# Prompt values of two query tiles in one portion, each head's first scores over 128 keys, and one tile's taps a pair later

## The chip, the cores and the metric

The kernel runs on one core of a Trainium2 chip. A core has a matrix engine (PE, with its weight loads shown apart as PEld), a vector engine (DVE), a scalar engine (ACT), GpSimd (POOL), SyncE (SP), which only issues transfers here, and 16 DMA engines. The metric is the device time of one execution in microseconds. Three runs of the kernel before took 966.77 to 967.02 us, with a median of 966.99 us.

## The reference

One layer of a hybrid decoder is computed for 512 prompt tokens (one sequence) and 8 sequences of 8 sample tokens. Two branches stand side by side, a short gated convolution and a sliding-window attention with 4 key heads of 4 query heads each. Then come a mix by gates, an output projection and a feed-forward part with a convolution of its own. What matters here:

```python
h = _rmsnorm(x, norm1_g) * (1.0 + sc1) + sh1
proj = h @ w_in
b_gate, c_gate, xa, q, k, v, ga, gb = jnp.split(proj, cuts, axis=-1)
u = c_gate * xa
uc, new_conv = _causal_conv(u, conv_buf, conv_w)      # three taps
ya = (b_gate * uc) @ w_conv_out
...
# attention, blocks of 128 queries against the block before and their own
s = einsum('...qhgd,...khd->...hgqk', q, k) * HEAD_DIM ** -0.5 - slope * dist
s = where(valid, s, NEG_INF)          # 0 <= dist <= 128, and no key before the first
m = maximum(max(s), sink);  p = exp(s - m);  p = p / (sum(p) + exp(sink - m))
o = einsum('...hgqk,...khd->...qhgd', p, v)
```

The first block of the prompt has no block before it, so its queries have 128 keys, while those of the other three blocks have 256.

## The kernel before, in words

All activations lie transposed, 128 channels by 576 tokens (512 of the prompt and 64 of the samples). A float32 product is made of float32r matmuls: both operands are split into a high part (ACT writes it as a rounded copy, `whi`, `hh`) and a low part (DVE subtracts, `wlo`, `hl`), and three products are summed in PSUM. A plain product goes through the channels in k-steps of 6 matmuls, each low or high pair once over tokens 0 to 255 and once over tokens 256 to 575 (`128x256` and `128x320` in the rows). From 231 us on most products are made in pairs instead (class `Job`): two output tiles are built from seven products of 288 tokens each, whose weights and operands are sums of the raw ones.

PSUM has two large tiles (`mm`) for products and four banks (`aux`) for all else, taken in turn.

In the stretch that the change touches, seven tiles of the convolution branch (the list `PLAIN`) and the queries and keys of the heads are made by plain products. Attention is woven in between them by a generator, `attention()`: after each k-step a budget is raised, and when it is full the generator runs on to its next `yield`. The text between two yields is called a portion here. There are 16 units, one for each head `hd` and each query tile `i` of 128 queries. Step n of the generator issues

- the scores of unit n (`prompt_scores`): per query head two float32r matmuls, whose stationary tile is 128 queries (the 64 rows of the high and the 64 of the low part of q, one above the other) and whose moving tile is the keys `kh` and then `kl`. Two banks take the four heads. DVE adds the distance term (L1108) and `softmax` follows on DVE and ACT;
- the values of unit n-3 (`prompt_values`): F32 matmuls with V as the stationary tile (L1136) into one bank, which ACT copies to `ot` (L1144). With `i` = 0 there is one key tile (the trace shows 4 records), otherwise two (8 records);
- the turn of unit n-2 (`prompt_turn`): 4 or 8 transposes of the probabilities into one or two banks, which ACT copies to `pt` (L1127).

The queries of head 1, 2 and 3 are made by products among the plain ones (`queries`). ACT scales the high part into `q` (L896), DVE makes `low` (L899), and a POOL transfer `q<-low` (L903) puts it into the other 64 rows. Only then can the scores start that use this `q`.

The order on PE is fixed by the code through the whole of this stretch. DVE and ACT are put in order by a scheduler from its own simulated times until the last plain tile, and from there on they too run as written (`pinned += [pe, act, dve]`). POOL and SP issue the transfers.

In the last plain tile (`at == len(PLAIN) - 1`) the operands of the first pair job are prepared, `jobs[0].prepare("BD")`: B and D are two of the weight operands of the pair, and a letter in the string says that this operand's low half is made by ACT and a POOL transfer (`wlo<-raw`) instead of DVE. `inner[6]` is the convolution of the last plain tile: one tap on ACT and two on DVE (`y<-pad,parT,y`). It runs before the third product of `jobs[0]`; its output is an operand of `jobs[2]`.

Of the kernel before, what the change touches and what calls it, by code (L numbers as in the profile page):

```python
# [16 lines left out]
P = 128  # L17
D = 1024
# [54 lines left out]
def step_kernel(ctx: ExitStack, tc: tile.TileContext, ins: dict, outs: list):  # L73
    nc = tc.nc
# [430 lines left out]
    par = cp.tile([88, P], F32, tag="par", name="par")  # L505
# [298 lines left out]
    for x in range(2):  # L804
        for y in range(2):
            c = slice(2 * y, 2 * y + 2)
# [33 lines left out]
    def vt(i):  # L840
        return V[i // 2][:, i % 2, :]
# [31 lines left out]
    HALF = (slice(0, 64), slice(64, 128))  # L873
    KS, QS, ready = {}, {}, {}
# [12 lines left out]
    def queries(t, ps=None):  # L887
# [55 lines left out]
        op=ALU.mult,  # L943
# [25 lines left out]
    ot = [wp.tile([P, 4, NT], F32, tag="oh", name=nm("o"), bufs=2) for _ in range(2)]  # L969
# [125 lines left out]
    def prompt_scores(hd, i):  # L1095
        w = 256 if i else P
        k0 = (i - 1) * P if i else 0
        ss = [slot("s", shape=[P, 2, 256]) for _ in range(2)]
        kh, kl = (x[:, k0 : k0 + 256] for x in KS[hd])
        for x in range(2):  # L1100
            S = aux()
            for e in range(2):
                q = QS[4 * hd + 2 * x + e][:, i * P : i * P + P]
                dst = S[:, e * 256 : e * 256 + 256]
                matmul(dst, q, kh, start=True, stop=False)
                matmul(dst, q, kl, start=False, stop=True)
            for e in range(2):
                nc.vector.scalar_tensor_tensor(  # L1108
                    out=ss[x][:, e, :w], in0=nd[:, 256 - w : 256],
                    scalar=2.0 ** (-8.0 * (4 * hd + 2 * x + e + 1) / 16),  # L1110
                    in1=S[:, e * 256 : e * 256 + w], op0=ALU.mult, op1=ALU.add,
                )
        softmax(ss, 4, snk[:, 4 * hd : 4 * hd + 4], nsnk[:, 4 * hd : 4 * hd + 4], w)
        return ss
# [13 lines left out]
            pts.append(t)  # L1128
        return pts

    def prompt_values(hd, i, pts):
        nkt = len(pts)
        O = aux()
        for n in range(2 * nkt):
            kt, par = n // 2, n % 2
            done = nc.tensor.matmul(  # L1136
                O[HALF[par], :256],
                vt(i - nkt + 1 + kt)[:, hd * 64 : hd * 64 + 64],
                pts[kt][:, par * 256 : par * 256 + 256],
                start=(kt == 0), stop=(kt == nkt - 1),  # L1140
            )
            if n:
                tc.keep_in_program_order(done)
        nc.scalar.copy(  # L1144
            ot[hd // 2][:, 2 * (hd % 2) : 2 * (hd % 2) + 2, i * P : i * P + P],
            O[:, :256].rearrange("p (g c) -> p g c", g=2),
        )

    def attention():
        units = [(hd, i) for hd in range(4) for i in range(4)]  # L1150
        s, pts = {}, {}
        for n in range(len(units) + 3):
            if n in CACHE_AT:
                cache_load(CACHE_AT.index(n))
            if n < len(units):
                hd, i = units[n]
                while 4 * hd + 3 not in QS or ticks[0] < ready[hd]:
                    yield False
                s[n] = prompt_scores(hd, i)
            yield False  # L1160
            if n >= 3:
                prompt_values(*units[n - 3], pts.pop(n - 3))
            if 2 <= n <= len(units) + 1:
                pts[n - 2] = prompt_turn(units[n - 2][1], s.pop(n - 2))
            yield False
        filler[1] = .35
        before = None
        for n in range(3):
            s, more = [], []
            if n < 2:  # L1170
                yield from decode_scores(n, s, more)
            if before is not None:
                yield from before
            before = decode_values(n, s, more)
# [228 lines left out]
    inner = {}  # L1403
# [7 lines left out]
    def gate_job(n):  # L1411
# [3 lines left out]
    jobs = [  # L1415
        branch(0, 1), branch(2, 4), branch(5, 6), gate_job(0), gate_job(1), gate_job(2), inner_job(3),
        inner_job(7), gate_job(3), branch(3, 7), gate_job(4), gate_job(5), gate_job(6), gate_job(7),
    ]
# [3 lines left out]
    hp = [PairOperands(h, kp, made, xn) for kp in range(4)]  # L1422
# [6 lines left out]
    for at, m in enumerate(PLAIN):  # L1429
        if at in (4, 5):  # L1430
            src, dst = ((ins["cache_k_win"], nks), (ins["cache_v_win"], nvs))[at - 4]
# [12 lines left out]
        w = weights(kpm(w_in, 1024 + m * P), NK)  # L1444
# [13 lines left out]
        w = weights(kpm(w_in, 2048 + m * P), NK)  # L1458
# [4 lines left out]
            jobs[0].load()  # L1463
        if at == len(PLAIN) - 1:
            pinned += [pe, act, dve]
            fs = [f for x in jobs[0].prepare("BD").values() for f in x]
            for k, n in [(0, 2), (1, 1), (2, 1), (3, 1), (4, 2), (5, 1), (6, 1), (7, 1)]:
                steps[k], fs = fs[:n], fs[n:]
            jobs[1].load()
        ps = product(w, h, steps)  # L1470
        u = padded()
# [17 lines left out]
    def g_list(names):  # L1489
        return [g_at(int(n[0]), n[1:]) for n in names.split()]  # L1490

    jobs[0].before = {2: [op.n3 for op in hp], 3: [lambda: inner[6]()]}
    jobs[7].before = {2: [lambda: inner[3]()]}
    jobs[8].before = {2: [lambda: inner[7]()]}
    jobs[9].before = {2: [lambda: state_out(NK, ncv_p[:], ncv_s[:])]}
# [516 lines left out]
    for m0, m1 in FCH:  # L2012
# [31 lines left out]
        if m1 < NF:  # L2044
# [3 lines left out]
            n = m1 - m0  # L2048
# [47 lines left out]
    jobs = [Job(w_dn[FB * P :, :], m * P, made3, lambda m=m: mix_outs(m, 40)) for m in range(0, NK - LATE, 2)]  # L2096
# [139 lines left out]
```

## Time and profile before

| what | value |
|---|---|
| median of three runs | 966.99 us |
| the profiled execution | 968.06 us, its span 966.2 us |
| mean granted TensorE clock | 0.996 |
| PE busy | 950.6 us (98%) |
| DVE busy | 710.5 us (74%) |
| ACT busy | 540.9 us (56%) |
| POOL busy | 131.8 us (14%) |
| share of PE in the chain that ended last | 94% |

The times in the profile are of the profiled execution, and us in a timeline count from the start of its span. A row of a timeline has the start, the duration, the engine, the line, the operation with what it writes and reads (output on the left of `<-`), the shapes, how many instructions were put together, and in brackets the idle time of the engine ahead of it with what ended it. The duration of a matmul includes its way through the array, and matmuls overlap. So what a matmul costs is read from the start of one to the start of the next, and not from its duration. F32 matmuls leave two records for each instruction.

### The profile page before, as it was taken

What the parts mean: (1) busy time and instruction counts of PE and PEld (TensorE: products, weight loads), DVE (VectorE), ACT (ScalarE), POOL (GpSimd) and SP (SyncE); (2) the same over time, 40 slices, a digit from 0 to 9 for tenths busy, and PEclk for the clock granted to TensorE, in tenths of its full rate; (3) what the DMA queues carried; (4) which work ended last, traced back from release to release, by engine and by line L of the source; (5) the groups of instructions that cost most, each with busy time, mean ns of one, the idle gap of its engine ahead of it and who ended that gap; (6) DMA issues with size and microseconds to landing.
All of it is one profiled execution on the core that took longest, in us unless ns stands there. A gap on an engine that the chain in (4) does not pass through costs nothing.

```text
span 966.2 us, 18732 instructions
## 1 busy us (share of the span) xinstructions
PE 950.6 (98%) x7326; PEld 913.5 (95%) x7326; DVE 710.5 (74%) x1330; ACT 540.9 (56%) x1021; POOL 131.8 (14%) x310
## 2 busy tenths in 40 slices
PE   7999999999999999999999999999999999999997
PEld 5799999898899989999889999999999999999997
DVE  4746777687865767876677688995559998968873
ACT  4454665558665446876335567564226565546664
POOL 2222112101211112210001131100000011101110
PEclk8999999999999999999999999999999999999999
DMA  9985332424655768899885742332333333328542
GB/s 276 326 253 147 90 85 71 130 87 119 154 139 160 242 215 214 209 248 268 300 285 131 169 109 66 89 103 73 101 91 93 88 88 103 89 78 175 131 90 99
DMA packets 182794, 144.61 MB, mean 150 GB/s; under 512 B 7704, under 2 KB 162140, under 8 KB 182418
## 3 DMA queue, kind: packets, MB, share of 16 engines
q1 hardware_dynamic: 172546, 111.72, 38.9%
q0 software_dynamic: 10016, 31.44, 14.3%
q8 instruction: 57, 0.93, 0.4%
q14 instruction: 31, 0.25, 0.1%
q10 hardware_dynamic: 144, 0.26, 0.1%
HBM read 113.89 MB, written 12.07 MB: 130 GB/s over the span
## 4 chain that ended last, share of the span: by engine, by line
PE 94%; DVE 2%; DMA 1%; ACT 1%; issue 0%; SPq 0%; POOL 0%; POOLq 0%; DVEq 0%; ACTq 0%
PE mm L112 54%; PE aux L112 37%; PE aux L1232 2%; PE aux L1136 1%; DMA x<-in_x_prompt 1%; DMA q<-low 1%; SPq L497 0%; DVE wlo L112 0%; ACT whi L112 0%; DVE s L1048 0%; ACT hh L112 0%; DVE raw L112 0%; ACT junk L112 0%; DVE hl L112 0%; DVE y L112 0%
## 5 line engine op out<-in xcount | busy, mean ns | idle before, releaser
L112 ACT ACTIVATE whi<-raw 128x1024 fp32r<-128x1024 f32 (+3 forms) x183 | 185.7, 1022 | 104.0 <-PE mm L112 40.9
L112 DVE TENSOR_TENSOR wlo<-raw,whi 128x1024 fp32r<-128x1024 f32 (+3 forms) x159 | 187.3, 1184 | 45.9 <-ACT whi L112 45.1
L112 PE MATMUL mm<-hh,whi 128*128 128x256 f32 x336 | 74.0, 301 | 0.5 <-ACT hh L112 0.5
L112 PE MATMUL mm<-hh,wlo 128*128 128x256 f32 x336 | 71.6, 294 | 0.0
L112 PE MATMUL mm<-hl,whi 128*128 128x256 f32 x336 | 70.8, 295 | 0.1
L112 PE MATMUL aux<-2l,whi 128*128 128x288 f32 (+2 forms) x232 | 68.4, 295 | 0.0
L112 PE MATMUL aux<-2h,whi 128*128 128x288 f32 (+2 forms) x232 | 68.4, 295 | 0.0
L112 PE MATMUL aux<-2h,wlo 128*128 128x288 f32 (+2 forms) x232 | 68.3, 295 | 0.0
L112 DVE TENSOR_TENSOR raw<-raw 128x512 f32<-128x512 f32 x82 | 57.8, 705 | 2.7
L112 PEld LDWEIGHTS mm<-hh,whi 128*128 128x128 f32 x336 | 55.1, 188 | 1.9 <-ACT hh L112 1.1
L112 PEld LDWEIGHTS mm<-hh,wlo 128*128 128x128 f32 x336 | 56.2, 188 | 0.0
L112 PEld LDWEIGHTS mm<-hl,whi 128*128 128x128 f32 x336 | 55.5, 188 | 0.7 <-DVE hl L112 0.5
L112 PE MATMUL aux<-hh,whi 128*128 128x288 f32 (+2 forms) x184 | 53.9, 300 | 0.0
L112 PE MATMUL aux<-hl,whi 128*128 128x288 f32 (+2 forms) x184 | 52.9, 294 | 0.0
L112 PE MATMUL aux<-hh,wlo 128*128 128x288 f32 (+2 forms) x184 | 52.8, 294 | 0.0
L112 PE MATMUL mm<-nh,whi 128*128 128x288 f32 x164 | 48.9, 298 | 0.2 <-DVE g L112 0.2
L112 PE MATMUL mm<-th,whi 128*128 128x288 f32 x164 | 49.1, 300 | 0.0
L112 PE MATMUL aux<-th,whi 128*128 128x288 f32 x164 | 48.6, 296 | 0.0
L112 PE MATMUL mm<-th,wlo 128*128 128x288 f32 x164 | 48.5, 295 | 0.0
L112 PE MATMUL aux<-th,wlo 128*128 128x288 f32 x164 | 48.4, 295 | 0.0
L112 PE MATMUL mm<-nl,whi 128*128 128x288 f32 x164 | 48.4, 295 | 0.0
L112 PE MATMUL mm<-nh,wlo 128*128 128x288 f32 x164 | 48.4, 295 | 0.0
(374 smaller groups left out, 3015.5 us busy)
## 6 DMA issues: line engine op xcount, KB each, us to landing
raw<-in_w_in SPq DMA_DIRECT2D x52, 512.0 KB, 4.9
raw<-in_w_up SPq DMA_DIRECT2D x44, 512.0 KB, 4.0
ada<-in_w_ada SPq DMA_DIRECT2D x64, 256.0 KB, 5.3
wlo<-raw POOLq DMA_DIRECT2D x18, 512.0 KB, 4.6
ad<-in_w_ada SPq DMA_DIRECT2D x32, 256.0 KB, 6.6
raw<-in_w_down SPq DMA_DIRECT2D x16, 512.0 KB, 4.2
sg_dram<-sg POOLq DMA_DIRECT2D x16, 288.0 KB, 4.3
gt<-sg_dram SPq DMA_DIRECT2D x16, 288.0 KB, 5.5
```

Source lines behind the costliest of these rows:

```text
L112: done = getattr(self.engine, name)(*args, **kwargs)
L1136: done = nc.tensor.matmul(O[HALF[par], :256], vt(i - nkt + 1 + kt)[:, hd * 64 : hd * 64 + 64], pts[kt][:, par * 256 : par * 256 + 256], st ...
L1232: done = nc.tensor.matmul(ps[32 * j : 32 * j + 32, :], cT[:, k, :], cols[k][j], start=(k == 1), stop=(k == NK - 2),)
```

## The change

Three things change.

1. `prompt_scores` of a unit with `i` = 0 uses the 128 keys it needs as the moving tile, instead of 256 of which it used 128. This touches 8 matmuls in each of the 4 heads.
2. `prompt_values` takes a list of units. It is called every second step, from n = 4 on, with units n-4 and n-3, two query tiles of the same head. Both go into one bank, columns 0 to 255 and 256 to 511. The two copies on ACT follow behind all matmuls.
3. In the last plain tile the low half of B of `jobs[0]` is made by DVE, and the convolution `inner[6]` runs before the third product of `jobs[1]` instead of `jobs[0]`.

```diff
--- before.py
+++ after.py
@@ -1096,12 +1096,12 @@
         w = 256 if i else P
         k0 = (i - 1) * P if i else 0
         ss = [slot("s", shape=[P, 2, 256]) for _ in range(2)]
-        kh, kl = (x[:, k0 : k0 + 256] for x in KS[hd])
+        kh, kl = (x[:, k0 : k0 + w] for x in KS[hd])
         for x in range(2):
             S = aux()
             for e in range(2):
                 q = QS[4 * hd + 2 * x + e][:, i * P : i * P + P]
-                dst = S[:, e * 256 : e * 256 + 256]
+                dst = S[:, e * 256 : e * 256 + w]
                 matmul(dst, q, kh, start=True, stop=False)
                 matmul(dst, q, kl, start=False, stop=True)
             for e in range(2):
@@ -1128,23 +1128,25 @@
             pts.append(t)
         return pts
 
-    def prompt_values(hd, i, pts):
-        nkt = len(pts)
+    def prompt_values(parts):
         O = aux()
-        for n in range(2 * nkt):
-            kt, par = n // 2, n % 2
-            done = nc.tensor.matmul(
-                O[HALF[par], :256],
-                vt(i - nkt + 1 + kt)[:, hd * 64 : hd * 64 + 64],
-                pts[kt][:, par * 256 : par * 256 + 256],
-                start=(kt == 0), stop=(kt == nkt - 1),
+        for u, (hd, i, pts) in enumerate(parts):
+            nkt, c = len(pts), slice(256 * u, 256 * u + 256)
+            for n in range(2 * nkt):
+                kt, par = n // 2, n % 2
+                done = nc.tensor.matmul(
+                    O[HALF[par], c],
+                    vt(i - nkt + 1 + kt)[:, hd * 64 : hd * 64 + 64],
+                    pts[kt][:, par * 256 : par * 256 + 256],
+                    start=(kt == 0), stop=(kt == nkt - 1),
+                )
+                if u + n:
+                    tc.keep_in_program_order(done)
+        for u, (hd, i, pts) in enumerate(parts):
+            nc.scalar.copy(
+                ot[hd // 2][:, 2 * (hd % 2) : 2 * (hd % 2) + 2, i * P : i * P + P],
+                O[:, 256 * u : 256 * u + 256].rearrange("p (g c) -> p g c", g=2),
             )
-            if n:
-                tc.keep_in_program_order(done)
-        nc.scalar.copy(
-            ot[hd // 2][:, 2 * (hd % 2) : 2 * (hd % 2) + 2, i * P : i * P + P],
-            O[:, :256].rearrange("p (g c) -> p g c", g=2),
-        )
 
     def attention():
         units = [(hd, i) for hd in range(4) for i in range(4)]
@@ -1158,8 +1160,8 @@
                     yield False
                 s[n] = prompt_scores(hd, i)
             yield False
-            if n >= 3:
-                prompt_values(*units[n - 3], pts.pop(n - 3))
+            if n >= 4 and n % 2 == 0:
+                prompt_values([(*units[u], pts.pop(u)) for u in (n - 4, n - 3)])
             if 2 <= n <= len(units) + 1:
                 pts[n - 2] = prompt_turn(units[n - 2][1], s.pop(n - 2))
             yield False
@@ -1463,7 +1465,7 @@
             jobs[0].load()
         if at == len(PLAIN) - 1:
             pinned += [pe, act, dve]
-            fs = [f for x in jobs[0].prepare("BD").values() for f in x]
+            fs = [f for x in jobs[0].prepare("D").values() for f in x]
             for k, n in [(0, 2), (1, 1), (2, 1), (3, 1), (4, 2), (5, 1), (6, 1), (7, 1)]:
                 steps[k], fs = fs[:n], fs[n:]
             jobs[1].load()
@@ -1489,7 +1491,8 @@
     def g_list(names):
         return [g_at(int(n[0]), n[1:]) for n in names.split()]
 
-    jobs[0].before = {2: [op.n3 for op in hp], 3: [lambda: inner[6]()]}
+    jobs[0].before = {2: [op.n3 for op in hp]}
+    jobs[1].before = {3: [lambda: inner[6]()]}
     jobs[7].before = {2: [lambda: inner[3]()]}
     jobs[8].before = {2: [lambda: inner[7]()]}
     jobs[9].before = {2: [lambda: state_out(NK, ncv_p[:], ncv_s[:])]}
```

The order on PE changes in the values and in the shapes of the scores only. In its rows `V` is the value tile, `pt` the transposed probabilities, `s` the scores that are transposed and `ident` the identity; the number behind a name tells one buffer from another, and `x2` means two instructions. The first place is on PE at step n = 4 of the generator (104.6 us in the profile). Before:

```order
L112 MATMUL mm_1355<-hh_352,wlo_1352 128x256
L112 MATMUL mm_1355<-hh_352,wlo_1352 128x320
L1136 MATMUL aux_1368<-pt_1270,V_683 64x256 x2
L112 MATMUL aux_1372<-ident,s_1119 128x128
L112 MATMUL aux_1372<-ident,s_1120 128x128
```

The two value matmuls of the first unit stand between a product and the transposes. The same place on PE now:

```order
L112 MATMUL mm_1355<-hh_352,wlo_1352 128x256
L112 MATMUL mm_1355<-hh_352,wlo_1352 128x320
L112 MATMUL aux_1368<-ident,s_1119 128x128
L112 MATMUL aux_1368<-ident,s_1120 128x128
L112 MATMUL aux_1368<-ident,s_1119 128x128
```

The values are gone, and the product is followed by the transposes at once. On PE one step later, n = 5 (112.4 us), where scores, values and transposes meet, stood before:

```order
L112 MATMUL aux_1449<-kh_1100,q_1337 128x256
L112 MATMUL aux_1449<-kl_1101,q_1337 128x256
L1136 MATMUL aux_1492<-pt_1377,V_683 64x256 x2
L1136 MATMUL aux_1492<-pt_1384,V_683 64x256 x2
L112 MATMUL aux_1498<-ident,s_1195 128x128
L112 MATMUL aux_1498<-ident,s_1196 128x128
L112 MATMUL aux_1498<-ident,s_1195 128x128
L112 MATMUL aux_1498<-ident,s_1196 128x128
L112 MATMUL aux_1449<-kh_1100,q_1338 128x256
```

There were four value matmuls, those of the second unit. And now on PE:

```order
L112 MATMUL aux_1445<-kh_1100,q_1337 128x128
L112 MATMUL aux_1445<-kl_1101,q_1337 128x128
L1137 MATMUL aux_1488<-pt_1270,V_683 64x256 x2
L1137 MATMUL aux_1488<-pt_1373,V_683 64x256 x2
L1137 MATMUL aux_1488<-pt_1380,V_683 64x256 x2
L112 MATMUL aux_1497<-ident,s_1195 128x128
L112 MATMUL aux_1497<-ident,s_1196 128x128
L112 MATMUL aux_1497<-ident,s_1195 128x128
L112 MATMUL aux_1497<-ident,s_1196 128x128
L112 MATMUL aux_1445<-kh_1100,q_1338 128x128
```

The values of the first unit have come to stand ahead of the second's, in the same bank (`aux_1488`), and the scores around them move 128 columns.

The second place is on DVE ahead of `low`, the low part of the last query tile of head 3, from 173 to 179 us in the profile. `den` belongs to the softmax, `nmx` is the negated maximum, L994 scales the probabilities, and `wlo` is the low half of a weight tile. Before:

```order
L991 TENSOR_TENSOR den_2146<-den_2146,es_2147 128x4
L992 RECIPROCAL den_2146<-den_2146 128x4
L1108 SCALAR_TENSOR_TENSOR s_2233<-con_919,aux_2235 128x256 x2
L994 TENSOR_SCALAR s_2126<-s_2126,den_2146 128x256 x2
L994 TENSOR_SCALAR s_2127<-s_2127,den_2146 128x256 x2
L1108 SCALAR_TENSOR_TENSOR s_2234<-con_919,aux_2242 128x256 x2
L975 TENSOR_REDUCE nmx_2249<-s_2233 128x2
L975 TENSOR_REDUCE nmx_2249<-s_2234 128x2
L112 TENSOR_TENSOR wlo_2800<-raw_2797,whi_2799 128x1024
L899 SCALAR_TENSOR_TENSOR low_2279<-mm_2183,q_2280 64x512
```

One scaling stands on each side of an addition to the next scores (L1108). On DVE now:

```order
L991 TENSOR_TENSOR den_2137<-den_2137,es_2138 128x4
L992 RECIPROCAL den_2137<-den_2137 128x4
L994 TENSOR_SCALAR s_2117<-s_2117,den_2137 128x256 x2
L994 TENSOR_SCALAR s_2118<-s_2118,den_2137 128x256 x2
L1108 SCALAR_TENSOR_TENSOR s_2229<-con_919,aux_2231 128x256 x2
L1108 SCALAR_TENSOR_TENSOR s_2230<-con_919,aux_2238 128x256 x2
L975 TENSOR_REDUCE nmx_2245<-s_2229 128x2
L975 TENSOR_REDUCE nmx_2245<-s_2230 128x2
L978 TENSOR_TENSOR nmx_2245<-nmx_2245,nsnk 128x4
L112 TENSOR_TENSOR wlo_2790<-raw_2787,whi_2789 128x1024
L981 TENSOR_TENSOR es_2250<-snk,nmx_2245 128x4
L899 SCALAR_TENSOR_TENSOR low_2275<-mm_2174,q_2276 64x512
```

Both scalings have moved ahead of both additions, and `es` (a small addition) ahead of `low`.

The third place is on DVE in the last plain tile and the first pair jobs, from 226 us on. The preparation of `jobs[0]` before:

```order
L112 TENSOR_TENSOR s_2921<-raw_2912,raw_2914 128x512
L112 TENSOR_TENSOR raw_2914<-raw_2914 128x512
L112 TENSOR_TENSOR wlo_2925<-raw_2912,whi_2924 128x1024
L112 TENSOR_TENSOR raw_2912<-raw_2912,raw_2914 128x512
L112 TENSOR_TENSOR raw_2912<-raw_2912 128x512
L112 TENSOR_TENSOR wlo_3003<-raw_2912,whi_3002 128x1024
```

Its DVE makes two low halves. On DVE now:

```order
L112 TENSOR_TENSOR s_2914<-raw_2905,raw_2907 128x512
L112 TENSOR_TENSOR raw_2907<-raw_2907 128x512
L112 TENSOR_TENSOR wlo_2918<-raw_2905,whi_2917 128x1024
L112 TENSOR_TENSOR wlo_2948<-raw_2907,whi_2947 128x1024
L112 TENSOR_TENSOR raw_2905<-raw_2905,raw_2907 128x512
L112 TENSOR_TENSOR raw_2905<-raw_2905 128x512
L112 TENSOR_TENSOR wlo_2994<-raw_2905,whi_2993 128x1024
```

The second `wlo` in a row is the low half of B. Further on DVE, behind the low parts `hl` of the operands, stood before the taps of `inner[6]`, and behind them the output `g` of the first pair:

```order
L112 TENSOR_TENSOR hl_434<-xn_390,hh_433 128x288
L975 TENSOR_REDUCE nmx_3182<-s_3097 128x2
L112 SCALAR_TENSOR_TENSOR y_3124<-pad_3018,parT,y_3124 128x592 x2
L112 TENSOR_TENSOR raw_2916<-raw_2916,raw_2918 128x512
L112 TENSOR_TENSOR raw_2916<-raw_2916 128x512
L112 TENSOR_TENSOR g_3028<-aux_3030,y_1096 128x288
```

The taps are the row `x2`. They have moved to here on DVE, behind a softmax in the second pair job:

```order
L991 TENSOR_TENSOR den_3172<-den_3172,es_3173 128x4
L992 RECIPROCAL den_3172<-den_3172 128x4
L994 TENSOR_SCALAR s_3088<-s_3088,den_3172 128x256 x2
L994 TENSOR_SCALAR s_3089<-s_3089,den_3172 128x256 x2
L112 SCALAR_TENSOR_TENSOR y_3266<-pad_3009,parT,y_3266 128x592
L112 TENSOR_TENSOR g_3204<-aux_3206,y_2010 128x288
L112 SCALAR_TENSOR_TENSOR y_3266<-pad_3009,parT,y_3266 128x592
L112 TENSOR_TENSOR raw_3015<-raw_3015,raw_3017 128x512
```

One tap stands on each side of that pair's first `g`, ahead of the next `raw` sum.

## The prediction

> **What bounds the kernel now.** I read the page's busy line first, then the chain of work that ended last.
>
> ```profile
> PE 950.6 (98%) x7326; PEld 913.5 (95%) x7326; DVE 710.5 (74%) x1330; ACT 540.9 (56%) x1021; POOL 131.8 (14%) x310
> PE 94%; DVE 2%; DMA 1%; ACT 1%; issue 0%; SPq 0%; POOL 0%; POOLq 0%; DVEq 0%; ACTq 0%
> ```
>
> PE sets the time: it is busy for 98% of the span and holds 94% of the chain. So each term below is a question of PE: does a step there become shorter, or does a wait of PE go or come? Work on DVE, ACT and POOL counts only where PE waits for it. As matmuls overlap, I cost them from start to start in the timeline. A measurement of this kernel can tell about 0.2% from no change, which is 1.93 us.
>
> **Values merged: eight islands fewer.** The timeline of PE, at a place without values, then at the values of step 4 and of step 5:
>
> ```profile
> 116.49 0.42 PE L112 MATMUL mm<-hh,wlo 128*128 128x256 f32 x2
> 116.75 0.60 PE L112 MATMUL aux<-ident,s 128*128 128x128 f32 x4
> 117.10 0.51 PE L112 MATMUL mm<-hh,whi 128*128 128x256 f32 x2
> ...
> 104.62 0.65 PE L1136 MATMUL aux<-pt,V 128*64 128x256 f32 x4
> 105.20 0.98 PE L112 MATMUL aux<-ident,s 128*128 128x128 f32 x7
> ...
> 112.29 0.28 PE L112 MATMUL aux<-kh,q 128*128 128x256 f32 x1
> 112.41 0.28 PE L112 MATMUL aux<-kl,q 128*128 128x256 f32 x1
> 112.62 1.08 PE L1136 MATMUL aux<-pt,V 128*64 128x256 f32 x8
> 113.63 0.66 PE L112 MATMUL aux<-ident,s 128*128 128x128 f32 x4
> 114.04 0.36 PE L112 MATMUL aux<-kh,q 128*128 128x256 f32 x1
> ```
>
> A burst of 4 value records takes 105.20 - 104.62 = 0.58 us, one of 8 takes 113.63 - 112.62 = 1.01. That is 0.11 for a record and about 0.15 for the burst itself. Going in costs too: the last float32r matmul takes 112.62 - 112.41 = 0.21 instead of 0.12, which is 0.09 more. Going out, the four transposes take 114.04 - 113.63 = 0.41, against 117.10 - 116.75 = 0.35 without values, 0.06 more. So an island costs 0.30 us beside its records. Sixteen become eight and the records stay the same (the group of values below counts 112: four units with 4, twelve with 8), so the term is 8 x 0.30 = **-2.4 us**. Bounds: nothing, if a unit's first matmul pays the 0.15 again inside a merged burst and the neighbours lose the rest, and -2.4.
>
> ```profile
> L1136 PE MATMUL aux<-pt,V 128*64 128x256 f32 x112 | 15.6, 394 | 0.0
> L1144 ACT COPY o<-aux 128x256 f32<-128x256 f32 x16 | 5.9, 370 | 13.8 <-PE aux L1136 13.7
> ```
>
> The 16 copies on ACT stay. Two now run behind one burst, so a bank comes free about 0.37 us later, every second step only; in the other steps a bank less is taken from the four. ACT is 56% busy and nobody reads `ot` inside this stretch, so I cost that at nothing. The cover is that idle time of ACT; without it, eight banks 0.37 us late would be at most +3.0.
>
> **Narrow scores.** Eight score matmuls in 256 columns, and the groups of all scores:
>
> ```profile
> 82.09 0.28 PE L112 MATMUL aux<-kh,q 128*128 128x256 f32 x1
> ...
> 82.93 0.28 PE L112 MATMUL aux<-kl,q 128*128 128x256 f32 x1
> ...
> L112 PE MATMUL aux<-kh,q 128*128 128x256 f32 x64 | 16.4, 286 | 0.7 <-DMA q<-low 0.7
> ```
>
> Seven steps take 0.84 us, 0.12 each. No float32r matmul of the trace moves fewer than 256 columns, so 128 columns have to be bounded by their neighbours:
>
> ```profile
> 566.72 0.80 PE L112 MATMUL aux<-ones,acc 128*128 128x2 f32 x6
> 567.38 0.36 PE L112 MATMUL mm<-2h,whi 128*128 128x256 f32 x1
> ...
> 237.96 0.49 PE L112 MATMUL aux<-kT,qS 64*128 64x128 f32 x4
> 238.38 0.40 PE L112 MATMUL mm<-th,whi 128*128 128x288 f32 x1
> ```
>
> The first row moves only 2 columns, yet with 128 weight columns its six take 0.66 us, 0.11 each. So there is a floor from the weight load, whatever is moved. Each score matmul loads a q tile of 128 columns, and I take 0.11: 32 x 0.01 = **-0.3 us**. The end below is the slope with the columns: the pair products of 288 columns step by 0.133 (0.80 us for six, rows below), which gives 0.07 at 128 and 32 x -0.05 = -1.6. The end above is plain F32 with 128 moving columns, the last group: two instructions, 4 records, in 0.42 us, so 0.21 for an instruction and 32 x 0.09 = +2.9. I stay with 0.11, because its row has the shape of the weights that the scores load. It is an assumption that float32r keeps its pace below 256 columns.
>
> The Trainium skill, "TensorE: Matmul & The Clock Gate", section "Back-to-back issue gap", gives about 81 ns for a sustained pair of weight load and matmul at 128 columns; by that the term would be -1.2 us, and the whole 0.9 us lower than mine. Its next section, "LDWEIGHTS (loading the stationary operand)", puts a load of 128 columns at 128/1.2, about 107 ns, which the 0.11 us here agrees with. The row decides, and I leave out the 81.
>
> **The wait of head 3.** PE waits once for `q<-low`: timelines of PE and DVE, and the chain between 180 and 186 us.
>
> ```profile
> 176.81 0.65 PE L1136 MATMUL aux<-pt,V 128*64 128x256 f32 x4
> ...
> 184.21 0.28 PE L112 MATMUL aux<-kl,q 128*128 128x256 f32 x1
> 185.15 0.36 PE L112 MATMUL aux<-kh,q 128*128 128x256 f32 x1 [0.66 <-DMA q<-low]
> ...
> 179.98 5.03 DMA q<-low
> ...
> 174.06 0.75 DVE L1108 SCALAR_TENSOR_TENSOR s<-con,aux 128x256 f32<-128x256 f32 x2 [0.65 <-PE aux L112]
> ...
> 178.77 0.67 DVE L899 SCALAR_TENSOR_TENSOR low<-mm,q 64x512 fp32r<-64x512 f32 x1
> ```
>
> The query product ends right ahead of the values at 176.81. From there two ways lead to the score at 185.15: PE's own, and over DVE's `low` (178.77) to the transfer. The island of 4 at 176.81 moves away, 0.58 + 0.15 = 0.73 us, so PE arrives 0.73 earlier at a transfer that doesn't, and this part of the gain goes into the wait. On the other side DVE, which is busy from 174.06 to `low`, had 0.65 us of idle time ahead of it; the scalings that are moved ahead can fill it, and `low` comes up to 0.65 earlier. The wait grows by 0.08 to 0.73. I take the middle, **+0.4**; the ends are -0.8 (a transfer as short as head 1's below, and the wait of 184.21 to 185.15 is gone) and +0.73. On POOL the `q<-low` has nothing new ahead of it.
>
> Heads 1 and 2 have the same pattern. In head 1 (POOL's timeline, and its transfer's time to landing):
>
> ```profile
> 106.84 0.52 POOL L903 DMA_DIRECT2D q<-low  x1 [6.38 <-DVE qX L907]
> ...
> q<-low POOLq DMA_DIRECT2D x1, 128.0 KB, 4.2
> ```
>
> It lands at 111.0 and the score that needs it starts at 112.29. Of these 1.3 us the removed island at 104.62 takes 0.73, so I cost it at nothing.
>
> **Taps and B's low half.** The waits of PE in the first pair jobs, then DVE there:
>
> ```profile
> 235.21 0.19 PEld L112 LDWEIGHTS aux<-th,wlo 128*128 128x128 f32 x1 [0.19 <-DMA wlo<-raw]
> ...
> 245.33 0.29 PE L112 MATMUL aux<-hh,wlo 128*128 128x288 f32 x1
> 245.85 0.40 PE L112 MATMUL mm<-nh,whi 128*128 128x288 f32 x1 [0.23 <-DVE g L112]
> ...
> 261.60 0.30 PE L112 MATMUL aux<-hh,wlo 128*128 128x288 f32 x1
> ...
> 262.40 0.29 PE L112 MATMUL aux<-th,wlo 128*128 128x288 f32 x1
> 263.11 0.40 PE L112 MATMUL aux<-kTc,qS 64*32 64x128 f32 x2 [0.41 <-DVE s L1048]
> ...
> 232.59 1.23 DVE L112 TENSOR_TENSOR wlo<-raw,whi 128x1024 fp32r<-128x1024 f32 x1 [2.01 <-ACT whi L112]
> ...
> 241.25 1.71 DVE L112 SCALAR_TENSOR_TENSOR y<-pad,parT,y 128x592 f32<-128x592 f32 x2
> ...
> 256.24 0.46 DVE L112 TENSOR_TENSOR g<-mm,p 128x288 f32<-128x288 f32 x1 [1.66 <-ACT kTc L1025]
> ...
> 262.58 0.87 DVE L1048 SCALAR_TENSOR_TENSOR s<-con,aux 128x256 f32<-128x256 f32 x2
> ```
>
> B's low half no longer comes by POOL's transfer, so PE's 0.19 at 235.21 goes: about -0.1. DVE pays 1.23 more (such a `wlo`), hidden in its idle 2.01 us ahead of 232.59; without that cover DVE would be late at the pad and later `hl`, up to +1.2. At 245.33 the step is 0.52 instead of 0.13: PE waits for `g`, and DVE is late with it because of the 1.71 us of taps at 241.25. They leave: -0.4. The taps land on DVE about where its idle 1.66 us ahead of 256.24 is, which hides them; with that gone, the `g` there would be up to 1.7 late. At 263.11 PE waits 0.41 for DVE's `s` at 262.58, behind a `wlo`. The addition now stands ahead of that `wlo`, but the taps are ahead of it too; I take half, -0.2. Together **-0.7**, bounds -0.9 and, if both covers fail, +2.
>
> **Sum.** -2.4 - 0.3 + 0.4 - 0.7 = -3.0 us. The profiled execution took 968.06 us (span 966.2), 1.07 above the median of the runs shown; so it would take 965.1, and the median 966.99 - 3.0 = **964.0 us**, 0.31% faster.
>
> **Rivals.**
> - *Float32r loses its pace at 128 columns.* For it: every float32r row moves 256 or more, and an F32 matmul of 128 columns takes 0.21. Against: nothing but that the format is the same. Then the scores are +2.9 instead of -0.3 and the sum is +0.2: 967.2 us, no change.
> - *The scores go as F32 in two loads each (slower).* The 0.21 above is for 64 rows of weights, with the two halves of the array side by side; the scores use all 128 rows, so nothing would run beside them and an instruction would cost two records after one another, 0.42. 32 x 0.30 = +9.6 instead of -0.3, in all +6.9: 973.9 us. It decides from 0.27 us a matmul on, where 32 x 0.15 = 4.8 eats 2.7 and 1.93 more. Against: PE would have to treat float32r as F32. The Trainium skill, "FP8 and Floating Point Precision", section "TensorE Precision Notes", says that true FP32 takes 4 passes through the array; it speaks of no width at which the reduced format would.
> - *The gain goes into waits.* The islands go, but heads 1 to 3 wait longer for `q<-low` (+0.7 each instead of +0.4 in all, +1.7) and the pair jobs keep theirs (+0.7): -0.6, 966.4 us. For it: the one wait that is there. Against: 1.3 us of room in head 1.
> - *The taps come late.* The covers in the pair jobs fail: +2 instead of -0.7, so -0.3, 966.7 us.
>
> **How the numbers follow.** The forecast has 0.56, its own range 962.2 (-2.4 - 1.6 + 0.08 - 0.9, the low ends) to 965.4 (-2.4 - 0.3 + 0.73 with the pair jobs at +0.4); float32r at a lower pace 0.20; as F32 0.11; waits 0.09; taps 0.04. Faster by over 0.2% (below 965.06) holds most of the forecast, 0.49, and a little of the rest, 0.03: 0.52. Slower is the F32 case and a tail of the lower pace, 0.14. The same is the rest, 0.34. The range has to reach over the lower pace at 967.2 and its spread: 962.2 to 968.6.
>
> **What would show it.** Islands of values: eight, of 12 or 16 records, 1.45 or 1.9 us long, and no burst at the place of 104.62. Scores of 128 columns: the start-to-start step, 0.11 or 0.21 or 0.42. The `q<-low` wait: 1 us or so, in head 3 alone. In the pair jobs, no wait for a transfer `wlo<-raw`, and none for `g` near 245. The prediction is wrong if the step of the scores is over 0.15, or if a new wait of PE for DVE or a bank stands at 80 to 265 us.

## The result and the profile after

Six executions of the changed kernel took 962.20 to 963.61 us, with a median of 962.91, beside 966.86 us for the kernel before. The ratio is 0.996 with an interval of 0.9947 to 0.9973: 3.95 us or 0.4% faster. A second comparison later gave 962.52 against 967.38 us, a ratio of 0.9946 (0.9934 to 0.9958). The prediction was 964.0.

The profiled execution took 963.13 us, its span 961.0. From the page, the busy line and the chain:

```profile
PE 946.4 (98%) x7326; PEld 912.7 (95%) x7326; DVE 711.9 (74%) x1331; ACT 539.1 (56%) x1020; POOL 132.3 (14%) x309
PE 95%; DMA 3%; SPq 1%; ACT 0%; DVE 0%; issue 0%; DVEq 0%
```

PE is still the bound. The timeline of PE in the changed kernel shows the steps of the change in the order of time:

```profile
82.34 0.22 PE L112 MATMUL aux<-kh,q 128*128 128x128 f32 x1
82.40 0.27 PE L112 MATMUL aux<-kl,q 128*128 128x128 f32 x1
...
83.18 0.49 PE L112 MATMUL mm<-hh,whi 128*128 128x256 f32 x2
83.50 0.43 PE L112 MATMUL mm<-hl,whi 128*128 128x256 f32 x2
...
104.48 0.42 PE L112 MATMUL mm<-hh,wlo 128*128 128x256 f32 x2
104.75 1.03 PE L112 MATMUL aux<-ident,s 128*128 128x128 f32 x8
...
112.02 1.52 PE L1137 MATMUL aux<-pt,V 128*64 128x256 f32 x12
113.46 0.65 PE L112 MATMUL aux<-ident,s 128*128 128x128 f32 x4
...
182.27 0.27 PE L112 MATMUL aux<-kl,q 128*128 128x128 f32 x1
182.86 0.30 PE L112 MATMUL aux<-kh,q 128*128 128x128 f32 x1 [0.32 <-DMA q<-low]
...
226.40 1.99 PE L1137 MATMUL aux<-pt,V 128*64 128x256 f32 x16
228.31 0.39 PE L112 MATMUL mm<-hh,whi 128*128 128x256 f32 x1
...
232.16 0.30 PE L112 MATMUL aux<-tl,whi 128*128 128x288 f32 x1
232.29 0.30 PE L112 MATMUL aux<-th,wlo 128*128 128x288 f32 x1
...
242.42 0.30 PE L112 MATMUL aux<-hh,wlo 128*128 128x288 f32 x1
242.55 0.29 PE L112 MATMUL mm<-nh,whi 128*128 128x288 f32 x1
...
259.02 0.29 PE L112 MATMUL aux<-th,wlo 128*128 128x288 f32 x1
259.24 0.68 PE L112 MATMUL aux<-kTc,qS 64*32 64x128 f32 x16
...
260.27 0.40 PE L112 MATMUL aux<-th,whi 128*128 128x288 f32 x1
```

Eight narrow scores take 0.84 us from 82.34 to 83.18, against 0.96 before (82.09 to 83.05), but the two product matmuls behind them take 0.32 to the next row instead of 0.26. At 104.75 the transposes follow the product at once. The 12 value records at 112.02 take 1.44, the 16 at 226.40 take 1.91. In the pair jobs the steps at 232.29 and 242.55 are 0.13 us, as if nothing were waited for, and the one at 259.24 is 0.22, as long as the same step at 256.66, where nothing is waited for.

The same matmuls in the timeline of before, to set the stretches against each other (82.09 and 263.11 are quoted above):

```profile
83.05 0.43 PE L112 MATMUL mm<-hh,whi 128*128 128x256 f32 x2
83.31 0.42 PE L112 MATMUL mm<-hl,whi 128*128 128x256 f32 x2
...
231.11 0.38 PE L112 MATMUL mm<-hh,whi 128*128 128x256 f32 x1
...
264.30 0.40 PE L112 MATMUL aux<-th,whi 128*128 128x288 f32 x1
```

| up to | before | after | gain in the stretch |
|---|---|---|---|
| the first score of head 0 | 82.09 | 82.34 | -0.25 (noise, nothing is changed there) |
| the first product behind the last values | 231.11 | 228.31 | 3.05 |
| behind the sample scores in the pair jobs | 264.30 | 260.27 | 1.23 |

Together 4.3 us between 82 and 264, with a median that is 3.95 lower. The profiled execution of before was 1.2 us above its median, so the two spans (966.2 and 961.0) overstate the gain.

### The profile page after: what moved, and what is told of

Its sections match the earlier page's. It is cut to its first block, busy times and chain, and to the rows that moved or that the text cites. A ratio compares the mean times of both kernels' runs of the same rounds, so it can differ in the third digit from the quotient of the medians.

```text
span 961.0 us, 18726 instructions
## 1 busy us (share of the span) xinstructions
PE 946.4 (98%) x7326; PEld 912.7 (95%) x7326; DVE 711.9 (74%) x1331; ACT 539.1 (56%) x1020; POOL 132.3 (14%) x309
## 4 chain that ended last, share of the span: by engine, by line
PE 95%; DMA 3%; SPq 1%; ACT 0%; DVE 0%; issue 0%; DVEq 0%
PE mm L112 55%; PE aux L112 37%; PE aux L1234 2%; DMA ad<-in_w_ada 1%; PE aux L1137 1%; DMA raw<-in_w_in 1%; SPq L497 1%; DMA q<-low 0%; ACT whi L112 0%; ACT wlo L112 0%; DVE cs L504 0%; ACT hh L112 0%; DVE hl L112 0%; DVE yo L112 0%; ACT acc L112 0%
## 5 line engine op out<-in xcount | busy, mean ns | idle before, releaser
L112 DVE TENSOR_TENSOR wlo<-raw,whi 128x1024 fp32r<-128x1024 f32 (+2 forms) x160 | 188.8, 1186 | 49.0 <-ACT whi L112 48.1
```

The lines of the kernel that those rows point to most:

```text
L112: done = getattr(self.engine, name)(*args, **kwargs)
```

## Experiments

All medians stand beside runs of the kernel before on the same chip. In the code below only the changed lines are shown; `...` stands for lines between them. The table has the differences of PE's starts at the same matmuls as above, against the first profile of before: in the stretch of the attention (80 to 231 us) and in the first pair jobs (231 to 265).

| kernel | median us | ratio (interval) | 80 to 231 | 231 to 265 |
|---|---|---|---|---|
| changed | 962.91 | 0.996 (0.9947 to 0.9973) | -3.0 | -1.2 |
| changed, again | 962.52 | 0.9946 (0.9934 to 0.9958) | -3.2 | -1.2 |
| values alone | 969.61 | 1.0019 (1.0009 to 1.0028) | -2.6 | +5.7 |
| scores alone | 967.46 | 1.0001 (0.9992 to 1.001) | +0.1 | 0.0 |
| taps and low half alone | 964.28 | 0.9974 (0.9965 to 0.9982) | +0.1 | -1.5 |
| low half alone | 966.68 | 0.9993 (0.9984 to 1.0002) | -0.9 | +0.6 |
| taps alone | 964.75 | 0.9973 (0.9964 to 0.9982) | -0.1 | -1.4 |
| changed without the low half | 967.48 | 0.9996 (0.9987 to 1.0004) | -3.1 | +4.4 |
| changed without the taps | 964.66 | 0.997 (0.996 to 0.998) | -2.2 | +1.0 |
| first scores in pieces of 64 keys | 966.34 | 0.9992 (0.9983 to 1.0) | 0.0 | -1.2 |
| values ahead of the scores | 964.40 | 0.9969 (0.9959 to 0.998) | -2.0 | -1.7 |
| values of four tiles | 966.68 | 0.9992 (0.9984 to 1.0001) | -0.1 | -0.8 |
| before, again (one execution) | 967.79 | | +0.2 | 0.0 |

### The values alone

Against the changed kernel:

```diff
-        kh, kl = (x[:, k0 : k0 + w] for x in KS[hd])
+        kh, kl = (x[:, k0 : k0 + 256] for x in KS[hd])
...
-                dst = S[:, e * 256 : e * 256 + w]
+                dst = S[:, e * 256 : e * 256 + 256]
...
-            fs = [f for x in jobs[0].prepare("D").values() for f in x]
+            fs = [f for x in jobs[0].prepare("BD").values() for f in x]
...
-    jobs[0].before = {2: [op.n3 for op in hp]}
-    jobs[1].before = {3: [lambda: inner[6]()]}
+    jobs[0].before = {2: [op.n3 for op in hp], 3: [lambda: inner[6]()]}
```

> Only the values of two units are merged; scores, taps and the low half of B stay as before. Theory (each of eight removed islands saves its 0.30 us, measured from start to start): -2.3 us, and head 3's wait for its query transfer changes as in the changed kernel, where the step before it shrank from 0.94 to 0.59 us: -0.3. In all -2.6 us. Rival (the saving is the head-3 wait and the neighbours of the scores, not the islands): under 1 us faster.

Neither happened: merging the values alone makes the kernel slower, by 1.8 us as the ratio has it (0.9 to 2.7 by its interval). The attention is 2.6 us shorter, as the theory had it: by PE's starts each two bursts of values that became one take 0.25 to 0.30 us less, 2.3 in all, and head 3's step shrinks from 0.94 to 0.64. But then PE comes to the first pair job, and what was a wait of 0.19 becomes one of 3 us. PE's timeline, the chain from 227 to 236 us and the granted clock by stretches (the third figure from the end of a row) of this kernel:

```profile
232.53 0.29 PE L112 MATMUL aux<-tl,whi 128*128 128x288 f32 x1
235.90 0.61 PE L112 MATMUL aux<-th,wlo 128*128 128x288 f32 x1 [3.08 <-DMA wlo<-raw]
...
238.12 0.44 PE L112 MATMUL aux<-tl,whi 128*128 128x288 f32 x1
238.36 0.44 PE L112 MATMUL aux<-th,wlo 128*128 128x288 f32 x1
...
241.88 0.30 PE L112 MATMUL mm<-tl,whi 128*128 128x288 f32 x1
242.01 0.30 PE L112 MATMUL mm<-th,wlo 128*128 128x288 f32 x1
```

```profile
230.77 5.09 DMA wlo<-raw
```

```profile
231.00:234.90 3.90, 1.82 (x15) 1.58 (x12) 2.91 (x5) 3.16 (x5) 1.94 (x6) 1.00 0.80 134
235.00:241.80 6.80, 5.90 (x38) 5.01 (x39) 1.59 (x3) 3.78 (x8) 1.45 (x2) 0.50 0.78 193
241.90:245.00 3.10, 3.10 (x24) 2.95 (x23) 3.10 (x8) 2.11 (x5) 0.85 (x1) 1.00 0.39 77
```

In the kernel before, the same transfer was issued at nearly the same time, by POOL's timeline:

```profile
230.49 0.97 POOL L112 DMA_DIRECT2D wlo<-raw  x1 [14.09 <-ACT wlo L112]
```

PE gains 2.5 us, but the transfer that brings B's low half leaves 0.3 us later than before, and it takes 5.1 us instead of 4.7. What holds it back is ACT, which writes `wlo<-whi` ahead of the transfer. ACT's timeline before:

```profile
226.96 1.06 ACT L1127 COPY pt<-aux 128x512 f32<-128x512 f32 x2
...
229.12 1.06 ACT L112 ACTIVATE wlo<-whi 128x1024 fp32r<-128x1024 f32 x1
```

And ACT's with the values merged:

```profile
227.43 0.58 ACT L1127 COPY pt<-aux 128x512 f32<-128x512 f32 x1 [2.22 <-PE aux L1137]
...
229.38 1.08 ACT L112 ACTIVATE wlo<-whi 128x1024 fp32r<-128x1024 f32 x1
```

Before, the last two copies into `pt` run one behind the other. Now the second waits for 2.22 us, until the merged value matmuls (L1137) are under way, although the transposes that it copies were done before 223 us, and `wlo<-whi` comes behind it. So the merge that brings PE 2.5 us earlier leaves ACT where it was. Probably the copy waits for a buffer that the values, now a step later, have still to read; no run tests this.

PE waits for the transfer from 232.53 to 235.90. That alone would give back the gain and 0.7 us more. But behind the wait the granted clock is 0.50: matmuls of 288 columns step by 0.24 us (238.12 to 238.36) instead of 0.13, until 241.88. That adds 2.6 us: at 235.90 this kernel is 0.69 us behind the kernel before (235.21), and at 241.88 it is 3.26 behind the same matmul there (238.62). So in this execution a wait that eats the gain takes as much again through the clock. The Trainium skill, "TensorE: Matmul & The Clock Gate", section "What's actually happening", names this: the clock is halved after at least one idle window of about 3.4 us, until there has been at least one busy window of that length, and the windows run freely. The half is as the trace shows it, and the 6.8 us at 0.50 are two such windows. But PE had been idle for only 2.2 us when the low clock began (the matmul at 232.53 ends at 232.82, the low clock begins at 235.0), so less than the page's window was enough here.

The twelve executions of this kernel lie in two groups, 967.0 to 968.3 us and 969.5 to 970.9 us; the profiled one (970.72) is of the upper. What parts them is not shown, since no lower one was profiled. A halved clock of 6.8 us can't be all of it: one execution of the upper group (970.21) has a mean granted clock of 0.998, which leaves room for less than 5 us at half.

### The changed kernel without the low half, and without the taps

```diff
-            fs = [f for x in jobs[0].prepare("D").values() for f in x]
+            fs = [f for x in jobs[0].prepare("BD").values() for f in x]
```

> The changed kernel, but the low half of B is made by ACT and the POOL transfer again. Theory (the merge brings PE some 2.5 us earlier to a transfer that does not come earlier; the wait costs 3.1 us and the lowered clock behind it another 2.4, as in the profile of the values alone): about 4 to 5 us slower than the changed kernel, so 0 to +1 us against the kernel before. Rival (the low half matters little, the taps give the gain): -3 to -4 us against the kernel before.

```diff
-    jobs[0].before = {2: [op.n3 for op in hp]}
-    jobs[1].before = {3: [lambda: inner[6]()]}
+    jobs[0].before = {2: [op.n3 for op in hp], 3: [lambda: inner[6]()]}
```

> The changed kernel, but the taps of the last plain tile run in the first pair job again. Theory (the taps made DVE late for the g and the s that PE waits for, 0.39 + 0.10 and 0.48 + 0.16 us by the two traces): 1.1 us slower than the changed kernel, -2.8 us against the kernel before. Rival (the taps give what the low half does not): 2 to 3 us slower than the changed kernel.

Without the low half the whole gain is gone: 967.48 us against 962.91 and 962.52. The timeline of PE shows the same wait and the same half pace (0.24 us from 237.21 to 237.45):

```profile
231.39 0.29 PE L112 MATMUL aux<-tl,whi 128*128 128x288 f32 x1
234.75 0.61 PE L112 MATMUL aux<-th,wlo 128*128 128x288 f32 x1 [3.07 <-DMA wlo<-raw]
...
237.21 0.44 PE L112 MATMUL aux<-th,wlo 128*128 128x288 f32 x1
237.45 0.44 PE L112 MATMUL aux<-th,whi 128*128 128x288 f32 x1
```

So the theory held, and the one word `"D"` for `"BD"` is worth 4.6 to 5 us by the medians (3.5 to 4.8 by the ratios), once the values are merged. Without the taps 1.8 to 2.1 us are lost, more than the theory's 1.1 and at the edge of the rival's 2 to 3. Here PE waits for `g` instead:

```profile
243.75 0.40 PE L112 MATMUL mm<-nh,whi 128*128 128x288 f32 x1 [1.32 <-DVE g L112]
```

This wait was 0.23 in the kernel before. DVE now also makes the low half (1.2 us), and PE comes earlier, so the 1.7 us of taps ahead of `g` weigh more than before. After these 1.3 us of idling the matmuls went on at 0.13 to 0.14 us: no halved clock.

### The low half alone, and the taps alone

> The kernel before, with the low half of B made by DVE. Theory (in the profile of before PE came 0.1 us too early for this transfer, and in other executions, where the transfer lands later, it waits longer and the clock falls): -1 to -2 us, more than the 0.2 us that the profile of before shows. Rival (the profile of before is what all executions do): -0.2 us.

> The kernel before, with the taps of the last plain tile one pair later. Theory (the two waits for DVE go): -1.1 us. With the -1 to -2 of the low half this makes the -2.95 us of both together. Rival (the taps give all of the -2.95 us): -2.7 us.

> Only the taps of the last plain tile run one pair later and the low half of B is made by DVE. Theory (the waits of PE at 235.2, 245.9 and 263.1 us of the profile before go whole): -1.0 to -1.2 us. Rival (those waits came with the later start of the values, and go with the merge): -0.3 us or nothing.

The edits are the two above, made in the kernel before, each alone and both together. The low half alone gives 0.7 us by the ratio, with an interval (-1.5 to +0.2) that includes no change and does not tell the theory from its rival. It removes 0.12 us at `wlo` and makes a longer wait for `g`, since DVE has 1.2 us more to do:

```profile
244.25 0.40 PE L112 MATMUL mm<-nh,whi 128*128 128x288 f32 x1 [0.84 <-DVE g L112]
```

The 0.9 us in the table at 80 to 231 are not the low half's: in this execution head 3 has no wait for its transfer.

The theory that other executions wait longer for the transfer falls: a second profile of before has the same stretch from 231 to 265 within 0.03 us, so there nothing changes from one execution to the other.

> The kernel before, once more, for a second profiled execution. Theory (PE's wait for the low half of B depends on when the transfer lands in that execution): the stretch from 231 to 265 us differs from the first profile by up to some us, and the wait for the query transfer of head 3 by some tenths. Rival (each execution does the same there): both within 0.1 us of the first profile.

The rival was right for the pair jobs. For the query transfer the theory was: in the second profile the step in head 3 is 0.27 us instead of 0.94.

```profile
184.97 0.28 PE L112 MATMUL aux<-kl,q 128*128 128x256 f32 x1
185.24 0.35 PE L112 MATMUL aux<-kh,q 128*128 128x256 f32 x1
```

The taps alone give 2.7 us by the median (1.7 to 3.5 by the interval), as the rival said. By the profile they give 1.4 us in the pair jobs, -0.39 and -0.10 at `g` and the rest at the sample scores. In the profiled execution another 0.8 us come between 600 and 890 us, where PE is busy throughout, waits for nothing, has a granted clock of 1.00, and its work is not changed. The taps don't explain it: the changed kernel has the same taps, and its steps in this stretch add up to what they were before. Both together gave no more than the taps alone, 2.5 us by the ratio (1.7 to 3.4), which is outside of the theory's 1.0 to 1.2; the profile has 1.5 in the pair jobs. With the taps alone and with both the profiled execution was slower than the median, by 0.8 and 2.0 us, so what the others gained beyond these 1.4 to 1.5 us is in no profile and stays open.

### The scores alone, and in pieces of 64 keys

```diff
-        kh, kl = (x[:, k0 : k0 + 256] for x in KS[hd])
+        kh, kl = (x[:, k0 : k0 + w] for x in KS[hd])
...
-                dst = S[:, e * 256 : e * 256 + 256]
+                dst = S[:, e * 256 : e * 256 + w]
```

> Only the first scores of each head move 128 columns. Theory (a floor of 0.11 us from the weight load, instead of 0.12): 32 x 0.01 = -0.3 us, and another -0.06 us for each head, because the first of eight steps at 128 columns took 0.06 in the changed kernel: -0.4 to -0.6 us in all. Head 3 gains nothing of it, as it waits for its transfer: -0.1 less. Rival (cost follows the columns): -1.6 us.

No difference can be measured; the interval (-0.8 to +1.0 us) rules out the rival's -1.6. By the trace, the burst of eight is 0.11 to 0.15 us shorter in each of the first three heads, the first product matmul behind each burst takes 0.05 longer, and in this execution head 3's wait for its `q<-low` was 1.1 us long, which takes it all back.

```diff
-                matmul(dst, q, kh, start=True, stop=False)
-                matmul(dst, q, kl, start=False, stop=True)
+                step = w if i else w // 2
+                for c in range(0, w, step):
+                    part = slice(c, c + step)
+                    matmul(dst[:, part], q, kh[:, part], start=True, stop=False)
+                    matmul(dst[:, part], q, kl[:, part], start=False, stop=True)
```

> The changed kernel with each of the 32 narrow score matmuls split into two of 64 keys: 64 matmuls instead of 32, the same columns. Theory (floor of 0.11 us from the load of 128 weight columns, whatever is moved): 32 x 0.11 = 3.5 us slower than the changed kernel, so -0.4 us against the kernel before. Rival (cost follows the columns): the time of the changed kernel, -3.9 us.

966.34 us, 3.4 to 3.8 more than the changed kernel. The timeline of PE has 16 matmuls of 64 columns in 1.71 us, 0.11 each:

```profile
82.47 0.19 PE L112 MATMUL aux<-kh,q 128*128 128x64 f32 x1
...
84.18 0.51 PE L112 MATMUL mm<-hh,whi 128*128 128x256 f32 x2
```

Half the columns cost the same, so the theory held and the floor of 0.11 us is not the columns'. That it is the load of the 128 weight columns is argued: no run changes their number. It is no cost of every matmul: with 32 weight columns (`kTc,qS`, 256.66 to 257.04 in the changed kernel) 16 records follow each other in 0.38 us.

### Values ahead of the scores, and values of four tiles

The first tries to use head 3's wait:

```diff
-                if u + n:
-                    tc.keep_in_program_order(done)
+                tc.keep_in_program_order(done)
...
+            if n >= 4 and n % 2 == 0:
+                prompt_values([(*units[u], pts.pop(u)) for u in (n - 4, n - 3)])
+            if n < len(units):
                 s[n] = prompt_scores(hd, i)
             yield False
-            if n >= 4 and n % 2 == 0:
-                prompt_values([(*units[u], pts.pop(u)) for u in (n - 4, n - 3)])
```

> The changed kernel, but in a step the values are issued ahead of the scores instead of behind them, and the values' first matmul too is held to this place. In head 3 the values of two units (12 records, 1.45 us) then stand ahead of the scores that wait for the transfer. Theory (the wait of 0.3 us in head 3 is PE coming early, and other work in its place costs nothing): 0.3 to 0.5 us faster than the changed kernel. Rival (the scores come 1.5 us later, DVE's softmax with them, and the wait moves to the transposes): the same as the changed kernel or slower.

1.5 to 1.9 us slower than the changed kernel, as the rival said. The wait in head 3 is gone, as PE's timeline shows (0.11 from 184.85 to 184.96), but a wait of the values for their `pt` has come, by PE's list of waits, and the values now stand apart from the transposes. In all the attention takes 1.1 us longer than in the changed kernel. Of this 0.4 stand in head 0's first scores, where PE waited for a query transfer in this execution; how much of the rest is the new edges of the islands was not measured apart.

```profile
183.02 1.51 PE L1137 MATMUL aux<-pt,V 128*64 128x256 f32 x12
...
184.85 0.27 PE L112 MATMUL aux<-kl,q 128*128 128x128 f32 x1
184.96 0.28 PE L112 MATMUL aux<-kh,q 128*128 128x128 f32 x1
```

```profile
PE aux L1137 <- ACT pt L1127: 0.4, 1, 0.4
```

The second goes on with the merge:

```diff
-            if n >= 4 and n % 2 == 0:
-                prompt_values([(*units[u], pts.pop(u)) for u in (n - 4, n - 3)])
+            if n >= 6 and n % 4 == 2:
+                for m in (n - 6, n - 4):
+                    prompt_values([(*units[u], pts.pop(u)) for u in (m, m + 1)])
```

> The changed kernel, but the values of all four query tiles of a head are issued in one portion, into two banks, every fourth step: four islands instead of eight. Theory (each island removed saves the 0.24 to 0.30 us that the merge of two saved): 1.0 to 1.2 us faster than the changed kernel. Rival (the probabilities are held longer and four copies follow one another on ACT, so a wait of PE for a bank or a buffer takes the place): no change or slower.

966.68 us, 4 more than the changed kernel, as the rival said. The first three heads gain nothing by it. Where both kernels have issued the values of three heads (84 records; the product matmul at 204.64 here, at 204.44 in the changed kernel), PE is 0.75 us later, counted from the first score of head 0. Head 0 loses 0.5 in its first scores, where PE waits for a query transfer in this execution, and then gains 0.2. In head 2 no values stand between the first scores any more, and PE waits there for the transfer of their queries:

```profile
149.23 0.30 PE L112 MATMUL aux<-kh,q 128*128 128x128 f32 x1 [0.81 <-DMA q<-low]
```

Then comes the last burst. Its last units need the `pt` that ACT has just begun to copy, and there is no other attention work left to put between:

```profile
225.01 2.38 PE L1137 MATMUL aux<-pt,V 128*64 128x256 f32 x20
229.60 1.14 PE L1137 MATMUL aux<-pt,V 128*64 128x256 f32 x8 [2.22 <-ACT pt L1127]
230.67 0.53 PE L112 MATMUL mm<-hh,whi 128*128 128x256 f32 x2
```

The product behind it starts 2.4 us later than in the changed kernel (230.67 against 228.31). A merge of four for the first three heads and of two for the last wasn't tried.

### The changed kernel again

> The changed kernel once more, beside the two below: -3.9 us against the kernel before, as the first time. PE's wait for the query transfer of head 3 between 0 and 0.7 us, as the landing varies from execution to execution.

962.52 us, 4.9 less than the kernel before beside it, with an interval (4.1 to 6.4) that overlaps the first one. In this profile head 3 has no wait for `q<-low` in the list. Over the profiles the transfer of head 3 took 3.96 to 5.41 us, and the wait 0 to 1.1.

## Why the prediction was right, and where it was wrong

The time, 962.9 against 964.0, lies in the range and on the side that was forecast. The reasons are half right.

- **Values merged, -2.4.** Measured in the changed kernel: 3.05 us in the attention, of which about 0.35 are the scores and 0.35 head 3, which leaves 2.35; with the values alone it was 2.3. The cost of an island, 0.15 of its own and 0.15 at its edges, was right. The cover beside it was not: "ACT is 56% busy and nobody reads `ot` inside this stretch, so I cost that at nothing". That looks at the copies behind a burst. The copies into `pt` ahead of it were left out, and there ACT stands still for 2.22 us (with the values alone at 227.43, in the changed kernel at 227.10).
- **Narrow scores, -0.3.** About 0.35 by the trace: the bursts are 0.12 shorter in head 0 and 0.15 in heads 1 and 2, since the first of the eight is followed after 0.06 only, and in each head 0.05 to 0.06 is lost again on the first product matmul behind them. The size of the floor was right: 0.11 at 128 columns and at 64 too. The row it was taken from was in part luck. Its six records are plain F32, three instructions in the code, so by instructions it gives 0.22; the prediction counted it by records, and the other F32 row, with 0.21, by instructions. Both rivals on the pace of float32r fall with the measured 0.11.
- **Head 3, +0.4.** The sign was wrong: the step with the wait went from 0.94 to 0.59 (182.27 to 182.86). DVE's `low` did come earlier, by 0.5 us against the product, but the transfer took 4.48 instead of 5.03 in that execution. The term was sized from one landing, and landings differ by 1.5 us over the profiles; in the same kernel before the step was 0.94 in one execution and 0.27 in the other.
- **Taps and B's low half, -0.7.** In the pair jobs 1.2 us were gained. All three waits went, the one ahead of the sample scores whole and not by half, though their burst itself (259.24 to 259.85) still takes 0.2 us longer than the same burst at 256.66. But the working of this step is what failed. The prediction wrote of the low half: "so PE's 0.19 at 235.21 goes: about -0.1". That is its worth with the values of before. With the values merged PE arrives 2.5 us earlier at that transfer, which ACT's wait keeps from coming earlier, and then the low half is worth 3.5 to 5 us; where the clock was halved (both profiles with the wait), nearly half of it is the clock's. The prediction had this argument in hand, for head 3, where it let PE arrive 0.73 us earlier at a transfer that doesn't; it did not carry the islands' whole gain on to the next transfer that PE meets. Likewise the taps: a step of 0.4 and one of 0.2 were counted, and in the changed kernel they are worth about 2 us, since DVE has the low half to make too and PE is earlier.
- **The sum.** It came out near the time because the change holds all parts together. As a sum of independent terms it is refuted: values alone +1.8, low half alone -0.7, taps alone -2.7, scores alone 0 (by the ratios and medians above), while all together give -3.95. The islands' gain reaches the end only because the low half no longer comes by a transfer.
- **Rivals.** "The gain goes into waits" named `q<-low`, where it didn't happen in the changed kernel. It does happen, in full, for a transfer that it didn't name, as soon as the low half is left out. The taps' covers held.

## What to carry to other kernels

When work is taken away from the bounding engine, follow its earlier arrival to the next operand that comes by a transfer. Ask by how much that operand is ahead, and whether what makes it moves forward too: here it was late already by 0.2 us, and the same merge made ACT, which prepares it, wait for PE, so none of the 2.5 us could pass. Parts of a change that look independent can be worth nothing or less alone; price each with the others made. And a wait on PE of some 3 us can cost more than itself.

## What the runs showed of the hardware

- A wait of PE of 3.1 us went with a granted clock of 0.50 for 6.8 us, in both kernels that had it: 235.0 to 241.8 us with the values alone, 234.1 to 240.8 without the low half. It began 2.2 and 2.4 us into PE's idling and ended some 6 us after PE went on. Waits of 0.8 and 1.3 us in the same pair jobs, and one of 2.2 (values of four tiles), left the clock at 1.00.
- A float32r matmul whose stationary tile has 128 columns takes 0.11 us from start to start at 64 and at 128 moving columns, and 0.12 at 256. At 128 the first of a burst takes 0.06, and the matmul behind the burst 0.05 to 0.06 more.
- A burst of F32 matmuls among float32r ones costs 0.25 to 0.30 us beside its records, and a second unit in the same bank hardly anything more: 16 records took 1.91 us in one burst (226.40 to 228.31), 8 took 1.01.
